# A hybrid encoder layer: TensorE of the first stage in written order, recurrence steps between thirds of projection blocks, five groups of tiles instead of six

## The chip, the core and the metric

The kernel runs on one NeuronCore of a Trainium2 chip. Its engines are TensorE (PE, with its weight loads as PEld), VectorE (DVE), ScalarE (ACT), GpSimd (POOL) and the DMA queues, of which SyncE (SP) and ScalarE issue most here. Each engine takes its instructions in order and waits at semaphores. The metric is device time in microseconds, the median of several executions. One execution was also recorded by the hardware profiler.

## What is computed

One layer of a streaming encoder, over 16 tiles of 128 frames of a new stream (tiles 0 to 15, "prompt") and one tile that holds the next 16 frames of 8 running streams (tile 16, "sample"). Cut to what matters:

```python
h = rmsnorm(x, norm_mix_pre)
P = h @ w_in                              # q, k, v, z (512 each), b, a (4 each), B, C, H (512 each)
qkv = silu(causal_dwconv(P[qkv], 4 taps)) # per channel along the frames
q, k = l2norm(q) / sqrt(128), l2norm(k)   # 4 heads of 128
# gated delta rule in chunks, S is a 128x128 state per head:
A  = strict_lower((k * beta) @ k.T * decay)
u, w = solve(I + A, [v * beta, k * beta * exp(g)])
v_new = u - w @ S
o  = (q * exp(g)) @ S + (q @ k.T * decay) @ v_new
S  = S * exp(g_last) + k_tail.T @ v_new   # the next chunk needs it
o  = rmsnorm_head(o) * silu(z)
y  = B * causal_dwconv(C * H, 3 taps)
x  = x + rmsnorm(concat(o, y) @ w_o)
x  = x + rmsnorm(SwiGLU(rmsnorm(x)))      # feed-forward, d_ff 2816
```

The chunks of the prompt are a sequence: each needs the state that the one before it leaves.

## The kernel before, in words

The work has stages: the first (projection by `w_in`, convolutions, delta rule, short convolution), the output projection by `w_o` (`o_tile`, matmuls at L818), the gate and up projections (L1034) and the down projection (L1192). Only the first and the loads of `o_tile` are touched.

**Groups and blocks.** The first stage runs over six groups of tiles, `[[0,1,16],[2,3,4],[5,6,7],[8,9,10],[11,12],[13,14,15]]`. Within a group the columns of all its tiles lie side by side (384, or 256), and the projection is 28 blocks of 128 output channels: 4 of k, 4 of v, 4 of q, 4 of z, and four times C, H, B. To keep float32 accuracy, operands are split into a high and a low part, and each block is 8 x 3 = 24 matmuls (`project`, `mm3`, L141). The weights of a block, split, are 1 MB; they are made from raw weights in the first use and kept in HBM (`weights`, L330 to L351), with three buffers on the chip.

**What follows a block.** For k, v and q (`conv_qkv`, L384 to L409): evacuate the bank (L376, in the first group L378, times the norm), copy the 3 columns of history (L393, L395), scale (L403, L405), three taps on DVE (L372), SiLU (L407), then one transposition per tile on TensorE (L428, L446, L457), and for k and q sums of squares (L413). For z a SiLU; for C, H, B products and two taps (`sc_stage`).

**Gates.** `gate_prep` makes decays and rates (Exp, Ln, Exp) and loads the decay matrices `dt` back from HBM (L319 to L325). They are scaled by the key norms in the v blocks (L451).

**The delta rule** of a group (`pair_stage`, `level_stage`, `chunk_stage`, `sample_stage`): key and query products per tile (L526, L527); the diagonal 32x32 blocks of A go to HBM (L535) and come back with one block per partition (L539); DVE inverts all of them in 31 steps of two operations (L546, L548); the result goes to HBM and back (L549, L551, L563, L569) and is joined to 128x128 inverses by small products (L575, L585, L586, L596, L601). Then, tile after tile, the recurrence: five products per tile (L641, L648, L655, L662, L667), the state update (L658), and the output's norm and transposition (`out_stage`, L624). The sample tile has products with the states of the 8 streams (L694, L696, L710).

**Order.** The program is written stage after stage, but the tile framework reorders: it lists the instructions of each engine by readiness in a timeline that it computes itself, with the written order as priority. The order on each engine is then fixed. So products of the levels and of the recurrence stand on TensorE among later projection blocks, and the last tile's recurrence of each group (`held`) is also written after the next group's inputs. Data of two groups are kept at a time (`gp`, `dp`; `dt` has 2 x 3 buffers).

**The next stage** loads `w_o` into buffers (`wor`, L794, then cast, L797, L798) that lie where the first stage's last buffers lay.

Of the kernel before, what the change touches and what calls it, by code (L numbers as in the profile page):

```python
# [9 lines left out]
F32 = mybir.dt.float32  # L10
# [7 lines left out]
P = 128  # L18
D = 1024
KD = D // P  # L20
H = 4
# [9 lines left out]
GROUPS = [[0, 1, 16], [2, 3, 4], [5, 6, 7], [8, 9, 10], [11, 12], [13, 14, 15]]  # L31
MAXT = max(len(g) for g in GROUPS)
W1 = MAXT * P
WF = W1 + NS * 3
# [3 lines left out]
NR, NKV = 3, 2  # L38
XKB = 4
NWB = 12  # L40
# [32 lines left out]
def kernel(  # L73
# [34 lines left out]
    mixd = [dram.tile([P, KD, P], F32, name=f"mixd{t}") for t in range(NT)]  # L108
# [37 lines left out]
    with ExitStack() as ph:  # L146
# [15 lines left out]
        S = gp.tile([P, H, P], F32, tag="S", name="S_init", bufs=2)  # L162
        V.memset(S, 0.0)
        junkq = gp.tile([P, P], BF16, name="junkq")
        junko = gp.tile([P, P], BF16, name="junko")

# [3 lines left out]
        dp = inner.enter_context(tc.tile_pool(name="dp", bufs=1))  # L170
        hp = inner.enter_context(tc.tile_pool(name="hp", bufs=KD + 3))
        wp = inner.enter_context(tc.tile_pool(name="wp", bufs=2))
        cp = inner.enter_context(tc.tile_pool(name="cp", bufs=2))

        def spread(r, n):
            c = n * P
            rg = cp.tile([P, W1], F32, tag="xk", name="rg", bufs=XKB)
# [8 lines left out]
        def x_prep(tiles):  # L186
            n = len(tiles)
            c = n * P
            ss = small.tile([P, MAXT], F32, tag="xss", name="xss")
            s2 = small.tile([P, MAXT], F32, tag="xs2", name="xs2")  # L190
            for i, t in enumerate(tiles):
                for q in range(2):
                    xt = cp.tile([P, D // 2], F32, tag="x", name="xt")
                    with tc.issue_after(wloads[-20 + 2 * i + q].ins):
                        nc.sync.dma_start(out=xt, in_=x[t, :, q * 512:(q + 1) * 512])
                    if q:
                        V.scalar_tensor_tensor(xt, xt, 1.0, xt, op0=ALU.mult, op1=ALU.mult, accum_out=s2[:, i:i + 1])
                    else:
                        A.activation(xt, xt, AF.Square, accum_out=ss[:, i:i + 1])
            V.tensor_add(ss[:, :n], ss[:, :n], s2[:, :n])  # L200
            r = rstd(small, ss[:, :n], n, 1.0 / D, EPS, "x")
            rb = spread(r, n)
            hi, lo = [], []
            for k in range(KD):
                xk = cp.tile([P, W1], F32, tag="xk", name="xk", bufs=XKB)
                with tc.issue_after(wloads[-11 + k].ins):
                    nc.sync.dma_start(out=xk[:, :c], in_=xT[k, :, tiles[0] * P:tiles[0] * P + c])
# [1144 lines left out]
```

## Time and profile before

| | us |
|---|---|
| median of 3 runs (2606.47 to 2608.23) | 2608.04 |
| span of the profiled execution | 2604.1 |
| start of groups 2 to 6 (their first projection matmul) | 171.3, 362.7, 518.6, 677.6, 801.2 |
| last projection matmul of the first stage | 955.9 |
| first matmul of the output projection | 969.8 |
| first matmul of the feed-forward | 1192.8 |

The span is from the first to the last instruction of the profiled execution; the runs were timed from outside. How to read the profile's lines: a group of instructions is given as line, engine, operation, `out<-in` by the program's names and shapes, then the count, busy time in microseconds and mean nanoseconds of one, and last the idle time of the engine just before them with what ended it. SPq and ACTq are instructions that issue DMAs. A row of a window gives the stretch, its length, and for each engine its busy time and number of instructions, then the granted clock of TensorE (1.00 is full speed), the DMA share and GB/s. Waits are put down to the semaphore that came last.

### The profile page before, as it was taken

The numbers are of one execution on the slowest core, as the hardware profiler recorded it, in microseconds if no ns is written. First come the engines' busy times: TensorE is split into PE (matmuls) and PEld (weight loads), VectorE is DVE, ScalarE is ACT, GpSimd is POOL, SyncE is SP. The second block draws the span as 40 slices with busy tenths as digits, with TensorE's granted clock in tenths as the row PEclk, the third lists the DMA queues.
The fourth block names the chain that finished last, engine by engine and source line by source line (L and its number), as shares of the span: only waits on it lengthen the run. The fifth ranks groups of instructions, "written<-read, shape, count | busy, mean of one in ns | idle before, by whom it ended". The sixth has DMA issues, their size and how long they took to land.

```text
span 2604.1 us, 41820 instructions
## 1 busy us (share of the span) xinstructions
PE 2507.8 (96%) x15061; PEld 2337.2 (90%) x15061; DVE 1741.0 (67%) x3502; ACT 1060.3 (41%) x2570; POOL 632.7 (24%) x580
## 2 busy tenths in 40 slices
PE   8989999999999999999999999999999999999998
PEld 7978899999888988788999999999999988787786
DVE  6876666666586655777888864544655554677588
ACT  6546145162656423444434442222433335333343
POOL 3221101010120101214556610000000035455563
PEclk9999999999999989999999999999999999999999
DMA  7966575847666564678877788877988853333465
GB/s 243 308 246 224 200 280 211 271 162 261 200 225 227 192 218 145 219 235 288 301 251 265 264 273 270 273 247 240 301 270 295 271 180 103 119 121 122 129 216 185
DMA packets 320815, 589.41 MB, mean 226 GB/s; under 512 B 55532, under 2 KB 204720, under 8 KB 301792
## 3 DMA queue, kind: packets, MB, share of 16 engines
q1 hardware_dynamic: 182512, 509.28, 57.8%
q10 hardware_dynamic: 138096, 77.46, 9.9%
q8 instruction: 119, 1.95, 0.3%
q14 instruction: 88, 0.72, 0.1%
HBM read 424.60 MB, written 162.05 MB: 225 GB/s over the span
## 4 chain that ended last, share of the span: by engine, by line
PE 67%; DVE 12%; DMA 10%; ACT 5%; issue 3%; POOL 2%; ACTq 1%; SPq 0%; DVEq 0%; POOLq 0%
PE fbank L1034 30%; PE dbank L141 15%; PE fbank L1192 11%; PE tbank L818 2%; PE dbank L818 2%; DMA xt<-in_x 1%; DMA xk<-in_xT 1%; DVE acc L372 1%; POOL dw L891 1%; ACT L407 1%; DVE Ts L548 1%; DVE pr L546 1%; DMA hTd<-ht 1%; DMA partd<-pt 1%; DMA out_y<-xr 1%
## 5 line engine op out<-in xcount | busy, mean ns | idle before, releaser
L1034 PE MATMUL fbank<-xh,fw 128*128 128x384 f32 (+1 forms) x3696 | 902.1, 327 | 9.2 <-ACT m L1068 5.1
L141 PE MATMUL dbank<-hi,w 128*128 128x384 f32 (+1 forms) x2688 | 689.3, 335 | 15.1 <-ACT w L344 6.2
L1034 PEld LDWEIGHTS fbank<-xh,fw 128*128 128x128 f32 x3696 | 653.7, 189 | 11.3 <-ACT m L1068 5.9
L1034 PE MATMUL fbank<-xl,fw 128*128 128x384 f32 (+1 forms) x1848 | 603.7, 327 | 0.0
L141 PEld LDWEIGHTS dbank<-hi,w 128*128 128x128 f32 x2688 | 482.1, 192 | 22.9 <-ACT w L344 6.6
L1192 PE MATMUL fbank<-dw,as 128*128 128x512 f32 x1980 | 460.7, 394 | 7.7 <-ACT dw L889 2.5
L1192 PEld LDWEIGHTS fbank<-dw,as 128*128 128x128 f32 x1980 | 371.6, 188 | 96.5 <-DVE as L1176 3.7
L141 PE MATMUL dbank<-lo,w 128*128 128x384 f32 (+1 forms) x1344 | 446.7, 332 | 0.1
L1034 PEld LDWEIGHTS fbank<-xl,fw 128*128 128x128 f32 x1848 | 348.7, 189 | 0.0
L141 PEld LDWEIGHTS dbank<-lo,w 128*128 128x128 f32 x1344 | 257.1, 191 | 3.3 <-issue 1.2
L1176 POOL TENSOR_TENSOR as<-ar,as 128x256 fp32r<-128x256 f32 (+1 forms) x207 | 186.7, 912 | 281.9 <-ACT as L1173 281.1
L1151 DVE TENSOR_TENSOR acc<-acc,fbank 128x512 f32<-128x512 f32 x248 | 166.3, 682 | 93.6 <-PE fbank L1192 77.9
L891 POOL TENSOR_TENSOR dw<-dr,dw 128x512 fp32r<-128x512 f32 x52 | 77.0, 1493 | 483.7 <-ACT dw L889 483.5
L1173 ACT CAST as<-ar 128x256 fp32r<-128x256 f32 (+1 forms) x288 | 118.1, 427 | 186.2 <-PE fbank L1192 133.8
L1009 ACT CAST fw<-rg 128x512 fp32r<-128x512 f32 x124 | 77.4, 624 | 190.5 <-PE fbank L1034 156.5
L372 DVE SCALAR_TENSOR_TENSOR acc<-R,cw,acc 128x384 f32<-128x384 f32 (+2 forms) x216 | 132.4, 617 | 11.4 <-ACT acc L403 7.7
L346 POOL TENSOR_TENSOR w<-wr,w 128x512 fp32r<-128x512 f32 x49 | 71.7, 1464 | 240.1 <-ACT w L344 189.8
L1081 DVE TENSOR_TENSOR c<-u,fbank 128x384 f32<-128x384 f32 (+1 forms) x66 | 34.9, 528 | 102.1 <-PE fbank L1034 102.1
L1077 DVE TENSOR_TENSOR m<-m,m 128x384 f32<-128x384 f32 (+1 forms) x44 | 23.1, 526 | 98.2 <-ACT m L1070 98.1
L344 ACT CAST w<-wr 128x512 fp32r<-128x512 f32 x98 | 56.5, 615 | 69.9 <-PE dbank L141 27.1
L546 DVE TENSOR_TENSOR pr<-As,Ts 48x31 f32<-48x31 f32 (+25 forms) x186 | 66.3, 356 | 26.4 <-DMA As<-sa 22.1
L1079 ACT ACTIVATE m<-fbank 128x384 f32<-128x384 f32 (+1 forms) x66 | 31.3, 474 | 121.4 <-PE fbank L1034 114.5
(360 smaller groups left out, 3697.2 us busy)
## 6 DMA issues: line engine op xcount, KB each, us to landing
w<-wsplit SPq DMA_DIRECT2D x119, 1024.0 KB, 5.7
fw<-fsplit SPq DMA_DIRECT2D x188, 512.0 KB, 4.6
fsplit<-fw SPq DMA_DIRECT2D x94, 512.0 KB, 4.9
partd<-pt ACTq DMA_DIRECT2D x88, 384.0 KB, 5.9
rg<-in_w_gu SPq DMA_DIRECT2D x62, 512.0 KB, 3.9
wsplit<-w SPq DMA_DIRECT2D x28, 1024.0 KB, 5.5
wr<-in_w_in SPq DMA_DIRECT2D x98, 256.0 KB, 3.4
ar<-partd SPq DMA_DIRECT2D x48, 384.0 KB, 3.5
```

The source lines that it names most:

```text
L141: T.matmul(ps, l, r, start=(i == 0), stop=(i == n - 1))
L346: e.tensor_tensor(out=wl[:, c], in0=wr, in1=wh[:, c].bitcast(F32), op=ALU.subtract)
L372: V.scalar_tensor_tensor(acc, raw(d), w[:, d:d + 1], acc, op0=ALU.mult, op1=ALU.add)
L546: V.tensor_mul(p3, As[:m, j, j + 1:32].unsqueeze(2).broadcast_to([m, a, b]), Ts[:m, j, 0:b].unsqueeze(1).broadcast_to([m, a, b]))
L818: T.matmul(pss[n], m_[:, j, :], w_[k][:, n * 512:(n + 1) * 512], start=(k == 0 and ci == 0), stop=(k == KD - 1 and ci == 2))
L891: e.tensor_tensor(out=w[:, 1], in0=v, in1=w[:, 0].bitcast(F32), op=ALU.subtract)
L1009: A.copy(w[:, 0], v)
L1034: T.matmul(ps, w_[:, c], b_[k][:, :hw], start=(first and k == 0 and ci == 0), stop=(k == KH - 1 and ci == 2), skip_group_check=not first)
L1151: V.tensor_add(dst, dst, ps)
L1173: ins = A.copy(a[:, 0, :n], v)
L1176: e.tensor_tensor(out=a[:, 1, :n], in0=v, in1=a[:, 0, :n].bitcast(F32), op=ALU.subtract)
L1192: T.matmul(ps, a[:, x_, q * P:(q + 1) * P], w[:, y_], start=(start and q == 0 and ci == 0), stop=(q == c - 1 and ci == 2), skip_group_chec ...
```

## The change

1. There are five groups, `[[0,1,16],[2,3,4,5],[6,7,8,9],[10,11,12,13],[14,15]]`. Three have four tiles, so that their matmuls have 512 columns; the last has two.
2. For the whole first stage TensorE's instructions keep the order in which they are written (`tc.manual_schedule` for PE alone). The other engines and queues are ordered by the framework as before.
3. The order of blocks in a group is k, q, one C-H-B, z, v, three C-H-B (`SEQ`). Each block is cut into thirds of 9, 9 and 6 matmuls, 84 thirds a group. `plan` writes each step of gates, pairs, solve, levels, recurrence and next inputs at a numbered third; what is numbered beyond 83 runs in the next group.
4. The transpositions of a block are written after the next block's matmuls (`laters`).
5. Products of the levels and the copies and trips around them are made for all tiles of a group at once. The decay is now one masked addition per tile and an exponential per head (with the row term as bias). The copies of history moved to POOL. Two operations of the normalization of the first group merged (`rb2`).
6. Buffers hold one group at a time (`kt`, `vt`, `kT`, `qT`, `U`, `AU`, `dt`); of the next group's normalized inputs two of eight have buffers before the group ends (`NHX`).
7. The mixed outputs are stored in two arrays, `mixo` per tile and `mixs` per group and channel block, and loaded by `o_tile` with two DMAs.

The core of the diff, new code:

```python
GROUPS = [[0, 1, 16], [2, 3, 4, 5], [6, 7, 8, 9], [10, 11, 12, 13], [14, 15]]
BLOCKS = [(kind, h) for kind in "kvqz" for h in range(H)] + [(kind, b) for b in range(4) for kind in "CHB"]
SEQ = [*range(0, 4), *range(8, 12), 16, 17, 18, *range(12, 16), *range(4, 8), *range(19, 28)]
...
def plan(g, nx, events):
    ...
    if gi:
        at(2, gate_products, g)
    at(5, gate_rates, g)
    at(11, gate_sums, g)
    at(14, gate_decay, g)
    at(16, key_norms, g)
    for i in range(n):
        at(17 + i, decay_exp, g, i)
        at(17 + i, decay_scale, g, i)
        at(21 + i, pair_keys, g, i)
        at(30 + 2 * i, pair_queries, g, i)
    at(21 + n, solve_load, g)
    for b in range(4):
        at(30 + 3 * b, solve, g, range(8 * b, min(31, 8 * b + 8)))
    at(40, solve_store, g)
    at(46, level_a, g)
    at(49, level_b, g)
    at(52, level_c, g)
    at(55, level_d, g)
    hop = 2 if n == MAXT else 3
    for i in range(npr):
        t = 60 + 3 * hop * i
        thread((t, t + hop, t + 2 * hop, t + 4 * hop), chunk(g, i))
    if npr < n:
        at(58, sample_start, g, npr)
        for h in range(H):
            t = 59 + 6 * h
            thread((t, t + 3, t + 5, t + 7, t + 9), sample_head(g, npr, h))
    ...
    if nx is not None:
        for i in range(len(tiles)):
            at(36 + 4 * i, x_rows, tiles, i, nx)
        at(54, x_spread, tiles, nx)
        for k in range(NHX):
            at(62 + 6 * k, x_norm, tiles, k, nx)
            at(63 + 6 * k, x_split, tiles, k, nx)
...
region.enter_context(tc.manual_schedule(engines={mybir.EngineType.PE}))
...
for gi, tiles in enumerate(GROUPS):
    ...
    for slot, j in enumerate(SEQ):
        jj, *w = pending.pop(0)
        early = gi == 0 and slot < 2
        ps = firsts[slot] if early else psd.tile([P, 512], F32, tag="d", name="dbank")
        for s, ks in enumerate((range(0, 3), range(3, 6), range(6, 8))):
            if not early:
                matmuls(ps, w, hi, lo, c, ks)
            if s == 2:
                later = finish_block(j, ps, g)
                fetch()
                if gi == 0 and slot == 0:
                    gate_products(g)
            for f in events.pop(3 * slot + s, ()):
                f()
        while laters:
            laters.pop()()
        if later:
            laters.append(later)
    if nx is not None:
        next_rows(gi + 1, nx)
        hi, lo, rb = nx["hi"], nx["lo"], None
    events = {t - 3 * len(SEQ): f for t, f in events.items()}
```

```python
def solve_store(g):
    n, m, As, Ts = g["n"], g["n"] * 16, g["As"], g["Ts"]
    nc.sync.dma_start(out=g["sT"][:n].rearrange("t h b j i -> (t h b) j i"), in_=Ts[:m])
    V.tensor_copy(As[:m].rearrange("p j i -> p i j"), Ts[:m])
    nc.sync.dma_start(out=g["sU"][:n].rearrange("t h b j i -> (t h b) j i"), in_=As[:m])
    utd = wk.tile([P, NS * (P + LS)], F32, tag="As", name="utd")
    ...
    for d, s in ((ud, "sU"), (td, "sT")):
        nc.sync.dma_start(out=d[:, :n].rearrange("p t h c -> p (t h) c"),
                          in_=g[s][:n].rearrange("t h b j i -> (b j) (t h) i"))

def level_a(g):
    n, npr, ud, td = g["n"], g["npr"], g["ud"], g["td"]
    for b in range(4):
        r = slice(32 * b, 32 * b + 32)
        A.copy(U[r, :n, :, r], ud[r, :n])
    ps = bank()
    for i in range(npr):
        for h in range(H):
            q = (4 * i + h) * 32
            for b in (0, 64):
                r1, r2 = slice(b, b + 32), slice(b + 32, b + 64)
                T.matmul(ps[r2, q:q + 32], AU[r1, i, h, r2], td[r1, i, h, :], start=True, stop=True)
    ...

def decay_exp(g, i):
    dt = g["dt"][i]
    for h in range(H):
        A.activation(dt[:, h, :], dt[:, h, :], AF.Exp, bias=g["nG"][:, 4 * i + h:4 * i + h + 1])

def chunk(g, i):                       # a generator: each yield ends a step of the plan
    ...                                # products with S: r, o; kl
    yield
    ...                                # U r, copied to yt
    yield
    ...                                # new state, o += QK yt, norm of o
    yield
    out_turn(g, i, o)                  # transposition, product with SiLU(z), store to mixo
    yield
```

More of the change, by code (lines that the diff above doesn't have):

```diff
@@ new lines, with fetch, matmuls @@
+        order = [(j, gi) for gi in range(len(GROUPS)) for j in SEQ]
+        pending = []
+        def fetch():
+            if order:
+                j, gi = order.pop(0)
+                pending.append((j, *weights(j, gi)))
+        def matmuls(ps, w, hi, lo, c, ks):
+            wh, wl = w
+            for k in ks:
+                for l, r in ((wh, hi), (wh, lo), (wl, hi)):
+                    T.matmul(ps[:, :c], l[:, k, :], r[k][:, :c], start=(k == 0 and r is hi and l is wh), stop=(k == KD - 1 and l is wl))
```

900 lines of the change are left out of this document (460 added, 440 removed).

## The prediction

> **What bounds the kernel now.** I read the page first, then the windows, cut where the first projection matmul of each group of tiles starts, then the timeline of TensorE and of the DMA issues around the small triangular solve.
>
> ```profile
> PE 2507.8 (96%) x15061; PEld 2337.2 (90%) x15061; DVE 1741.0 (67%) x3502; ACT 1060.3 (41%) x2570; POOL 632.7 (24%) x580
> ```
>
> ```profile
> 0.00:171.30 171.30, 148.57 (x824) 140.57 (x825) 137.78 (x349) 89.72 (x210) 54.24 (x46) 0.95 0.84 289
> 171.30:362.70 191.40, 180.42 (x1231) 167.31 (x1230) 128.18 (x325) 83.79 (x229) 21.82 (x24) 0.97 0.63 221
> 362.70:518.60 155.90, 154.19 (x1161) 149.41 (x1160) 96.08 (x272) 68.08 (x199) 10.69 (x12) 0.99 0.70 238
> 518.60:677.60 159.00, 155.92 (x1108) 149.91 (x1107) 101.69 (x278) 69.26 (x197) 11.71 (x12) 0.98 0.64 215
> 677.60:801.20 123.60, 114.71 (x964) 109.86 (x964) 96.61 (x272) 70.11 (x185) 26.60 (x22) 0.97 0.62 212
> 801.20:955.90 154.70, 148.59 (x1075) 142.43 (x1076) 89.56 (x252) 68.44 (x189) 7.47 (x9) 1.00 0.62 207
> 955.90:1192.80 236.90, 224.79 (x1173) 188.73 (x1173) 155.10 (x307) 93.59 (x233) 36.86 (x47) 0.96 0.61 198
> ```
>
> Columns: the stretch, its length, busy time of PE, PEld, DVE, ACT, POOL, granted clock, DMA share, GB/s. TensorE is the bound. The first stage takes 955.9 us, the output projection 236.9 more, up to the feed-forward's first matmul at 1192.8. The change can only move that 1192.8. Busy matmuls have modelled ends, so for the work I use the spacing in stretches that hold one kind only:
>
> ```profile
> 461.07:502.43 41.36, 41.36 (x241) 41.36 (x240) 30.32 (x87) 2.66 (x8) 0.00 (x0) 1.00 0.86 277
> 789.41:800.95 11.54, 11.54 (x95) 11.54 (x96) 9.35 (x27) 3.65 (x7) 1.29 (x1) 1.00 0.66 238
> 2305.03:2387.81 82.78, 82.78 (x365) 68.32 (x364) 59.60 (x90) 28.84 (x71) 44.74 (x50) 1.00 0.37 115
> ```
>
> They hold matmuls of 384, 256 and 512 columns: about 0.173, 0.122 and 0.227 us each. A block of 24 takes 4.15 us with three tiles, 2.92 with two and, from the last row (another stage's matmuls), 5.45 with four. One recurrence product is eight instructions:
>
> ```profile
> 293.90 1.06 PE L667 MATMUL obank<-yt,dt 128*128 128x128 f32 x8
> 294.79 1.06 PE L526 MATMUL gbank<-kT 128*128 128x128 f32 x8
> ```
>
> The next eight start 0.89 us later. Thus a group of three prompt tiles needs 28 x 4.15 = 116 us of projection and, for gates, transpositions (0.11 each), pairs, levels and recurrence, about 32: 148. The third and fourth stretches took 156 and 159. The waste is 5 to 7% there and more around the first group and the two-tile group. What keeps it low is that a solve and its recurrence may run late, under the next group's projections.
>
> **The change, part by part.** *Fewer, wider matmuls.* Before: 3360 x 0.173 + 672 x 0.122 = 663 us. After: 672 x 0.173 + 2016 x 0.227 + 672 x 0.122 = 656. It saves 7 us on the path.
>
> *Work off the path.* One solve fewer takes (67.8 + 66.3)/6 = 22 us from DVE (rows below), the edge copies move to POOL, and stores to HBM become fewer and larger. DVE is 67% busy and a matmul does not wait for these: I cost them at nothing. The POOL copies are not in the trace at this size; they can run before or behind the evacuation, so between 0 and, were they on each of 60 conv chains at a tenth of a microsecond, 6 us; I take 0.
>
> *The written order.* This is the part that counts. Within a group TensorE must now do, in this order: the k and q blocks, the key products (thirds 21 to 24), the rest of the projections, and at third 46 the first level, which needs the solve. Nothing behind it may pass, so a late solve stops the engine. I split a group into three legs.
>
> *Leg 2, from the last key product to the first level*, is a chain of a store, a load, 62 dependent DVE operations, two stores and two loads. The trace has it whole:
>
> ```profile
> 106.58 1.01 ACTq L535 DMA_DIRECT2D sa<-AU  x2
> ...
> 178.46 0.44 PE L575 MATMUL gbank<-utd,AU 32*32 32x32 f32 x16
> ...
> 749.71 0.39 ACTq L535 DMA_DIRECT2D sa<-AU  x1
> ...
> 812.60 0.44 PE L575 MATMUL gbank<-utd,AU 32*32 32x32 f32 x16
> ...
> 892.95 1.76 ACTq L535 DMA_DIRECT2D sa<-AU  x4
> ...
> 930.08 0.32 SPq L549 DMA_DIRECT2D sT<-Ts  x1
> ...
> 940.56 0.44 PE L575 MATMUL gbank<-utd,AU 32*32 32x32 f32 x16
> ```
>
> From the last tile's stores (its first issue, with two tiles its last) it takes 72 us in the first group, 63 with two tiles and 47.6 with the three of the last group. The solve's arithmetic is only this:
>
> ```profile
> L372 DVE SCALAR_TENSOR_TENSOR acc<-R,cw,acc 128x384 f32<-128x384 f32 (+2 forms) x216 | 132.4, 617 | 11.4 <-ACT acc L403 7.7
> L548 DVE TENSOR_TENSOR Ts<-Ts,pr 48x31 f32<-48x31 f32 (+25 forms) x186 | 67.8, 365 | 4.1
> L546 DVE TENSOR_TENSOR pr<-As,Ts 48x31 f32<-48x31 f32 (+25 forms) x186 | 66.3, 356 | 26.4 <-DMA As<-sa 22.1
> ```
>
> 31 x (0.365 + 0.356) = 22 us per group, however many tiles. The rest is DMA trips and other work of DVE between. In the new order the solve lies under the z blocks, where DVE has little else, so I take a little over the shortest row, 49 us with four and with two tiles, and 58 for the first group, whose weights are still split on DVE. Lower bound: the arithmetic and two trips like the last one in the rows (930.08, the solve's end, to 940.56), 43. Upper: the rows, with four tiles' larger trips 53: so 43 to 53, 43 to 63, 43 to 72. What TensorE has to do meanwhile (thirds 24, 23 and 22 to 46): four tiles, 22 x 5.45/3 = 40 plus 4 for query products and transpositions, 44; first group, 23 x 4.15/3 + 3 = 35; two tiles, 24 x 2.92/3 + 2 = 25. So it waits about 5, 23 and 24 us.
>
> *Leg 1, up to the last key product.* TensorE's work with four tiles is 8.4 blocks x 5.45 = 46, gate products 16 x 0.227 = 4, transpositions 3, key products 4 x 0.89 = 4: 57. Beside it stands ScalarE:
>
> ```profile
> L413 ACT ACTIVATE junkq<-tbank 128x128 bf16<-128x128 f32 x136 | 37.5, 276 | 13.4 <-PE tbank L457 6.5 <-DVE rg L178 1.5 <-DVE sqe L615 1.0
> L407 ACT ACT_TABLE_LOAD x27 | 34.6, 1283 | 0.8 <-DVE hist L395 0.3
> L403 ACT ACTIVATE acc<-dbank,cw 128x384 f32<-128x384 f32 x48 | 28.2, 587 | 0.1
> L413 ACT ACTIVATION_READ_ACCUMULATOR junkq<-tbank 128x1 f32 x136 | 27.1, 199 | 0.0
> L376 ACT COPY R<-dbank 128x384 f32<-128x384 f32 x48 | 22.7, 473 | 6.1 <-PE dbank L141 5.9
> L451 ACT ACTIVATE dt<-dt,c 128x128 f32<-128x128 f32 x68 | 20.9, 389 | 1.5 <-DVE c L437 1.5
> ```
>
> Per k or q block with four tiles: copy, scaling and SiLU, each about 0.6 (0.47 to 0.59 at 384 columns), four sums of squares of up to 0.475, for k one more copy: 3.2 to 4.4 us; eight blocks, 30. The decay is now 16 exponentials and 16 scalings of 0.3 to 0.39: 11. Some ten table loads (Exp, Ln and SiLU alternate) at 1.28: 13. Together 54 to 60 against 57. I take 59. The Trainium skill, "ScalarE: Activation LUTs", Terms, gives about 2.7 us for a table load; by that the leg would be some 14 us longer in each of five groups. The row says 1.28 and decides. With two tiles TensorE needs 28; ScalarE has 8 x 2 for the blocks, 5 for decays, 13 for tables, 5 for raw weights, 3 for others: 42. First group: the first two blocks wait for the loads as before, and DVE needs, per block, two evacuations (about 0.7 together), three taps of 0.62 to 0.73, a weight split (0.7 to 0.96) and edge copies: 4.4 to 4.6 for each 4.15 us block. Nine blocks and the start give 76.
>
> *Leg 3, from the first level to the group's end.* Four tiles: 12.25 x 5.45 = 67, levels 7, recurrence 4 x 5 x 0.89 = 18, the rest 4, and 4 for hops and the change of group, where six of eight normalized inputs wait for buffers of the block before: 100. First group, with the sample tile's 23 of products: 93. Two tiles: 12.25 x 2.92 = 36, levels 4, recurrence 9, rest 2, hops 3: 54.
>
> *The sum.* First group 76 + 58 + 93 = 227, three groups of 59 + 49 + 100 = 208 make 624, last 42 + 49 + 54 = 145: 996 against 955.9. But before, levels and recurrence of its last tiles ran after 955.9, about 20 us of products under the output projection's start:
>
> ```profile
> 956.93 0.92 SPq L794 DMA_DIRECT2D wor<-in_w_o  x2
> ...
> 969.85 0.77 PE L818 MATMUL dbank<-woh,mh 128*128 128x512 f32 x1
> ```
>
> Its weights can load only when the stage's buffers are free, and 14 us pass to its first matmul. After the change nothing is left to fill them, though DVE, then free, shortens them to about 10. The matmuls (17 tiles x 48 x 0.227 = 185) and transpositions (14) make 199; with 10 idle, 5 at a slow clock and 9 of later waits, as now, 223 instead of 236.9. So 996 + 223 = 1219 against 1192.8: **26 us longer**. The profiled span goes from 2604.1 to 2630; the median of 2608.04 lies 3.9 above the span, so 2634.
>
> **The rivals.** *B, the solve fits (faster).* If DVE serves the solve nearly without a break and the trips are at their short end, leg 2 falls to TensorE's own 44, 35 and 25, and no wait is left at the level: 3 x 5 + 23 + 24 = 62 us less, 2572. It speaks for it that 22 us of arithmetic and two trips of some 10 us fit 44; against it, none of the three rows is under 47 us, and two tiles have 25. It decides on the sign when the five waits together are under 36 us.
>
> *C, the transposition a block later comes too soon.* Now a block's transpositions may come late. After the change they stand one block behind, 5.9 us with four tiles; copy, scaling, three taps and SiLU take at least 0.6 + 0.7 + 2.3 + 0.6 = 4.2 (taps at 0.77, an estimate from 0.617). One other DVE and ScalarE operation in between is allowed, a table load with it is not. At 1.3 us more in 12 blocks of three groups it costs 45: 2679.
>
> *D, the clock.*
>
> ```profile
> PE tbank L141 <- DMA utd<-sT: 9.6, 1, 9.6
> ```
>
> ```profile
> 165.00:175.00 10.00, 4.03 (x13) 3.30 (x14) 5.04 (x10) 3.91 (x11) 2.35 (x4) 0.50 0.89 294
> ```
>
> The one long wait of now, 9.6 us on the solve's result, lies in a stretch with the clock at 0.50, and work after it ran at half speed for some 4 us. If each of five waits at the level does that, 2 to 3 us are lost each: 12 in all, 2646. The Trainium skill, "TensorE: Matmul & The Clock Gate", Part 1, says that an idle window of about 3.4 us throttles and about 3.4 us of activity releases; by it five waits lose five times 1.7, some 8 us.
>
> *E, the order is not what limits.* If the waits of before stay as they are, only 7 us of matmuls and a little at the start of the next stage change: 2597.
>
> **How the numbers follow.** Chances: the forecast 0.46, B 0.24, C 0.15, D 0.08, E 0.07. The forecast's own range, from the bounds of leg 2 (three times -5 to +4, -15 to +14, -6 to +14) with some of the errors cancelling, is 2610 to 2673. The range 2570 to 2680 takes in most of B and half of C. A measurement of this kernel tells 0.2%, 5 us, from no change. Faster by more: B and most of E, 0.30. Within: the rest of E and the forecast's low edge, 0.05. Slower: 0.65.
>
> **What would show it.** The 512-column projection matmuls should start 0.227 us apart. TensorE's largest waits should be at the first level (level_a), released by the load of the solved blocks, some 5 us with four tiles and over 15 in the first and last groups; if they are under 7 on average, B is right. Waits of the transpositions for SiLU of over 1 us in most k, v and q blocks would be C. The last projection should end near 996 and the feed-forward start near 1219. The prediction is wrong in its main step if the store-to-level chain takes under 42 us.

## The result, and the profile after

The changed kernel takes 2726.25 us (median of 4 runs, 2721.49 to 2729.33) against 2607.26 of the kernel before (4 runs, 2603.69 to 2608.23): ratio 1.0466, 95% interval 1.0447 to 1.0484. It is slower by 119 us; forecast were 26, and the range ended at 2680. The profiled execution's span is 2726.4 us, with a mean granted clock of 0.961 (0.984 before).

The page's first part, of the kernel after: busy time, share of the span, instructions.

```profile
PE 2509.9 (92%) x14366; PEld 2254.1 (83%) x14366; DVE 1672.9 (61%) x2986; ACT 1047.8 (38%) x2464; POOL 657.1 (24%) x724
```

TensorE is as long busy as before (2507.8) and the span is 122 us longer, so most of the loss is waiting. (The run no_order below shows that some of the busy time is loss too.) The prediction cut a group into three legs: to the last key product, to the first level, to the group's end. The windows of the kernel after, cut there (columns as before: stretch, length, PE, PEld, DVE, ACT, POOL, clock, DMA share, GB/s): leg 1 of the first group; the three legs of the third group; the three of the last.

```profile
7.60:88.30 80.70, 61.32 (x293) 54.65 (x294) 47.28 (x111) 52.91 (x136) 23.97 (x31) 0.83 0.56 198
...
479.80:560.20 80.40, 64.71 (x292) 49.66 (x291) 35.49 (x66) 55.88 (x148) 8.28 (x19) 0.89 0.46 157
560.20:613.00 52.80, 44.28 (x213) 36.86 (x213) 29.16 (x80) 8.81 (x24) 0.37 (x2) 0.95 0.66 205
613.00:711.40 98.40, 98.39 (x740) 84.09 (x741) 47.44 (x89) 25.10 (x60) 10.39 (x22) 0.97 0.45 153
...
943.00:999.30 56.30, 38.40 (x243) 34.65 (x243) 28.74 (x63) 38.51 (x103) 11.95 (x21) 0.79 0.43 145
999.30:1046.00 46.70, 25.73 (x215) 25.19 (x214) 30.33 (x78) 8.44 (x25) 4.61 (x7) 0.84 0.52 167
1046.00:1102.60 56.60, 53.32 (x518) 51.82 (x518) 33.07 (x61) 20.80 (x56) 13.27 (x21) 0.95 0.37 127
```

Beside the forecast, in us (the other groups of four tiles are within 3 of the third; the first group's leg 1 includes the 7.6 of the start):

| leg | forecast first / four tiles / last | measured |
|---|---|---|
| 1 | 76 / 59 / 42 | 88.3 / 83.1, 80.4, 80.8 / 56.3 |
| 2 | 58 / 49 / 49 | 59.5 / 52.8, 52.8, 52.7 / 46.7 |
| 3 | 93 / 100 / 54 | 98.0 / 98.1, 98.4, 98.1 / 56.6 |
| output projection | 223 | 214.7 |

Leg 1 is 94 us over its forecast, leg 2 is 10 and leg 3 is 2, and the output projection 8 under: together the 98 us by which the feed-forward starts late (1317.3 for 1219).

TensorE's waits in the kernel after (what waits, for whom: us in total, times, longest):

```profile
PE gbank L574 <- DMA utd<-sT: 68.0, 5, 23.9
PE tbank L325 <- ACT qT L318: 32.8, 7, 7.9
PE dbank L281 <- ACT hi L206: 31.4, 7, 7.2
PE tbank L325 <- ACT kT L318: 15.2, 11, 3.0
...
PE dbank L951 <- ACT mh L945: 9.8, 1, 9.8
```

The first row is the level (L574) waiting for the solved blocks: the 62 us of the forecast. `hi` (L206) is the next group's normalized input: 28 of the 31.4 us are the four changes of group, for which the sum had at most 4 each. `qT` and `kT` are SiLUs that a transposition (L325) waits for; the sum had nothing for them. The last row is the output projection's start, 9.8 for a forecast 10.

**The change of group.** SyncE's DMA issues at the end of the second group, in the kernel after (start, time over which they issue, line, what, count):

```profile
479.95 0.32 SPq L251 DMA_DIRECT2D w<-wsplit  x1
480.32 10.94 SPq L236 DMA_DIRECT2D xk<-in_xT  x6
```

The group's last matmuls run up to 479.8. The weight load needs the buffer that they free; the six input loads are written behind that load, so they issue after it, and the first is there at 486.5. TensorE waits 6.8 us, then for one split after another, and at half speed, as the granted clock of the stretch (0.50) shows:

```profile
485.40:495.40 10.00, 6.65 (x13) 3.93 (x13) 7.21 (x11) 3.99 (x6) 0.00 (x0) 0.50 0.45 153
```

The first block of the group takes 21.4 us (row below), of which matmuls at 0.227 us would fill 5.45 and gate products 3.6.

**The q blocks.** ScalarE's windows inside the third group's leg 1, kernel after (stretch, length, ACT busy, clock, DMA share, GB/s):

```profile
479.80:501.20 21.40, 7.06 (x17) 0.76 0.53 178
...
535.00:552.00 17.00, 16.88 (x50) 0.80 0.47 169
```

It is idle for two thirds of the first block and has no gap in the 17 us in which the second q block's SiLU is late. Its timeline there:

```profile
534.28 0.59 ACT L289 COPY R<-dbank 128x512 f32<-128x512 f32 x1 [2.13 <-POOL rt L506]
...
537.03 1.28 ACT L495 ACTIVATE dt<-dt,nG 128x128 f32<-128x128 f32 x4
...
544.09 1.28 ACT L318 ACT_TABLE_LOAD   x1
545.38 0.63 ACT L318 ACTIVATE qT<-acc 128x512 f32<-128x512 f32 x1
```

The second q block's SiLU (545.38) stands behind the decays, exponentials and scalings, from 537.03 on and two table loads; TensorE's transposition waits 6.0 us for it. VectorE in the same stretch:

```profile
536.15 1.35 DVE L490 TENSOR_TENSOR dt<-dt,cst 128x512 f32<-128x512 f32 x2 [4.09 <-DMA dt<-grow]
537.42 0.75 DVE L285 SCALAR_TENSOR_TENSOR acc<-R,cw,acc 128x512 f32<-128x512 f32 x1
...
541.12 0.69 DVE L490 TENSOR_TENSOR dt<-dt,cst 128x512 f32<-128x512 f32 x1 [1.67 <-DMA dt<-grow]
```

Mask additions that wait for the decay rows stand in front of the taps (L285) that the SiLU needs. So four causes could share leg 1: late loads, a chain of queues, ScalarE's load, or the written order as such. The experiments take them apart.

### The profile page after: what moved, and what is told of

The parts are those of the page before. It is cut to its first block, busy times and chain, and to the rows that moved or that the text cites. A ratio compares the mean times of both kernels' runs of the same rounds, so it can differ in the third digit from the quotient of the medians.

```text
span 2726.4 us, 39699 instructions
## 1 busy us (share of the span) xinstructions
PE 2509.9 (92%) x14366; PEld 2254.1 (83%) x14366; DVE 1672.9 (61%) x2986; ACT 1047.8 (38%) x2464; POOL 657.1 (24%) x724
## 4 chain that ended last, share of the span: by engine, by line
PE 72%; DVE 9%; DMA 8%; ACT 6%; issue 3%; POOL 1%; SPq 0%; ACTq 0%; DVEq 0%; POOLq 0%
PE fbank L1167 31%; PE dbank L281 16%; PE fbank L1325 12%; PE tbank L951 3%; PE dbank L951 3%; DMA xk<-in_xT 2%; DMA xt<-in_x 1%; DVE Ts L549 1%; DVE pr L547 1%; DMA sU<-As 1%; DMA utd<-sT 1%; ACT L318 1%; ACT dt L495 1%; ACT junkq L330 1%; PE tbank L325 1%
## 5 line engine op out<-in xcount | busy, mean ns | idle before, releaser
L281 PE MATMUL dbank<-hi,w 128*128 128x512 f32 (+2 forms) x2240 | 686.6, 379 | 40.8 <-ACT hi L206 31.4
L281 PEld LDWEIGHTS dbank<-hi,w 128*128 128x128 f32 x2240 | 427.4, 198 | 98.9 <-ACT hi L206 34.8
L281 PE MATMUL dbank<-lo,w 128*128 128x512 f32 (+2 forms) x1120 | 417.0, 372 | 4.6 <-DVE lo L207 4.6
L281 PEld LDWEIGHTS dbank<-lo,w 128*128 128x128 f32 x1120 | 222.2, 198 | 38.0 <-DVE lo L207 13.9
L285 DVE SCALAR_TENSOR_TENSOR acc<-R,cw,acc 128x512 f32<-128x512 f32 (+2 forms) x180 | 131.2, 730 | 97.0 <-ACT acc L314 91.4
L261 POOL TENSOR_TENSOR w<-wr,w 128x512 fp32r<-128x512 f32 x49 | 64.8, 1322 | 117.4 <-ACT w L259 110.0
L259 ACT CAST w<-wr 128x512 fp32r<-128x512 f32 x98 | 56.3, 616 | 57.1 <-PE dbank L281 31.3
L1143 POOL TENSOR_TENSOR fw<-rg,fw 128x512 fp32r<-128x512 f32 x44 | 69.5, 1579 | 30.8 <-ACT fw L1142 30.7
```

Source lines behind the costliest of these rows:

```text
L261: e.tensor_tensor(out=wl[:, c], in0=wr, in1=wh[:, c].bitcast(F32), op=ALU.subtract)
L281: T.matmul(ps[:, :c], l[:, k, :], r[k][:, :c], start=(k == 0 and r is hi and l is wh), stop=(k == KD - 1 and l is wl))
L285: V.scalar_tensor_tensor(acc, raw(d), w[:, d:d + 1], acc, op0=ALU.mult, op1=ALU.add)
L1143: e.tensor_tensor(out=w[:, 1], in0=v, in1=w[:, 0].bitcast(F32), op=ALU.subtract)
```

## The experiments

All times are medians; ratios are against the kernel before, timed on the same chip. The changed kernel stands at 2726.25.

| run | edit to the changed kernel | us | ratio, 95% interval |
|---|---|---|---|
| no_order | written order taken away | 2578.9 | 0.9891, 0.9869 to 0.9913 |
| no_order_six | no_order, six groups | 2625.3 | 1.0079, 1.0058 to 1.0099 |
| no_order_x | no_order, input loads earlier | 2575.2 | 0.9883, 0.9865 to 0.9901 |
| no_order_all3 | no_order, three edits | 2580.5 | 0.9911, 0.9890 to 0.9933 |
| x_early | input loads earlier | 2693.8 | 1.0337, 1.0308 to 1.0365 |
| q_lag2 | q transposed two blocks behind | 2698.6 | 1.0353, 1.0328 to 1.0378 |
| levels_later | levels six thirds later | 2698.4 | 1.0355, 1.0328 to 1.0383 |
| all3 | these three | 2641.7 | 1.0136, 1.0115 to 1.0156 |
| warm | matmuls in the level waits | 2716.0 | 1.0416, 1.0395 to 1.0437 |
| decay_pool | decay scalings on GpSimd | 2720.3 | 1.0445, 1.0426 to 1.0463 |
| gates_early | decay rows earlier | 2721.8 | 1.0445, 1.0413 to 1.0478 |
| silu_first | exponentials behind the SiLU | 2727.0 | 1.0461, 1.0445 to 1.0476 |
| q_chain | gates_early, silu_first, the power later | 2718.9 | 1.0441, 1.0418 to 1.0464 |
| q_chain_pool | q_chain and decay_pool | 2702.3 | 1.0372, 1.0352 to 1.0393 |
| all4 | all3 and gates_early | 2626.2 | 1.0084, 1.0061 to 1.0106 |
| all4_silu | all4 and silu_first | 2636.5 | 1.0110, 1.0090 to 1.0130 |

### Is it the written order?

```diff
-        region.enter_context(tc.manual_schedule(engines={mybir.EngineType.PE}))
```

> The written order of TensorE is taken away: the framework orders its instructions again as it does in the kernel before; the groups of four, the new stages and everything else of the change stay. Theory A (the written order is the loss: nothing behind a late step may pass): the waits at the first level (69.8 us), on late SiLUs (45) and much of the half-speed work (15) go, and the time comes to 2600 to 2640. Theory B (the first leg's loss comes from the new stages themselves, the late input loads and ScalarE in the q blocks, whatever the order): the level waits go, but the four group changes still cost some 9 us each and the rest of ScalarE's lateness stays: 2650 to 2690. Theory C (four tiles and single buffers are what makes it slow): 2700 or more.

2578.9: theory A, 21 us under its range, and 147 us less than with the order, more than the whole loss. TensorE's waits in no_order:

```profile
PE dbank L281 <- DMA w<-wsplit: 16.3, 12, 4.1
...
PE gbank L574 <- DMA utd<-sT: 5.1, 2, 4.0
PE tbank L325 <- ACT qT L318: 5.0, 4, 2.6
```

The level waits 5.1 us instead of 68, `qT` 5.0 instead of 32.8, and no row for `hi` is left among the large ones. TensorE's same 14366 instructions are busy for 2480.2 us here, 2509.9 in the kernel after: some 30 of the 152 us between the two spans are instructions that last longer. The lower clock in the kernel after (0.961 for 0.989) fits that; no run separates it. How it gets there is in the counts of projection matmuls (L281) between the starts of successive first levels. The windows of that line in no_order, and the first two of the same kind in the kernel after:

```profile
0.00:192.40 192.40, 145.26 (x716) 132.24 (x716) 0.96 0.78 268
192.40:401.00 208.60, 155.45 (x635) 117.10 (x634) 0.99 0.59 198
401.00:571.60 170.60, 126.53 (x505) 94.58 (x505) 0.97 0.53 182
571.60:760.80 189.20, 152.00 (x627) 114.92 (x626) 1.00 0.55 185
760.80:946.20 185.40, 136.95 (x880) 120.09 (x879) 1.00 0.54 182
```

```profile
0.00:147.70 147.70, 81.89 (x378) 74.19 (x378) 0.84 0.65 223
147.70:381.70 234.00, 154.73 (x672) 124.20 (x672) 0.94 0.58 192
```

At 24 to a block, the first level of the first group comes after 29.8 blocks in no_order and after 15.75 in the written order. Summed up, the later ones come after 56.3, 77.3, 103.5 and 140 blocks, against 43.75, 71.75, 99.75 and 127.75: 4 to 14 blocks later, different in each group. The written order's place is the same in every group and early.

### What are the five groups worth?

```diff
-GROUPS = [[0, 1, 16], [2, 3, 4, 5], [6, 7, 8, 9], [10, 11, 12, 13], [14, 15]]
-MAXT = max(len(g) for g in GROUPS)
+GROUPS = [[0, 1, 16], [2, 3, 4], [5, 6, 7], [8, 9, 10], [11, 12], [13, 14, 15]]
+MAXT = 4
```

> Without the written order and with the six groups of the kernel before (0 1 16, 2-4, 5-7, 8-10, 11-12, 13-15), in buffers still sized for four tiles; the new stages, stores and planned places stay. Theory 1 (the 26 us under before come from five groups: 7 us of wider matmuls and one solve, one group change and one first leg less): about 2600 to 2610, that is before's time. Theory 2 (they come from the other parts: edge copies on GpSimd, fewer stores, the new order of blocks): within 8 us of 2579.

2625.3, outside both theories: five groups are worth 46 us, not 26, and with six groups the other new parts, their plan and buffers made for five, cost about 20. TensorE's largest wait in no_order_six is for weights:

```profile
PE dbank L281 <- DMA w<-wsplit: 32.4, 17, 4.4
```

against 16.3 in no_order. That is about 16 of the 46; the rest was not told apart.

### The three places in the written order

x_early:

```diff
-            with tc.issue_after(wloads[-1].ins):
+            with tc.issue_after(wloads[-4].ins):
                 nc.sync.dma_start(out=xk[:, :c], in_=xT[k, ...])
```

> The loads of the next group's inputs that were queued on SyncE behind the newest weight load now follow a weight load three blocks older; nothing else changes. Theory (the group change is late because these six loads stand behind a weight load that itself waits for the group's last block): the first block of each later group, now 21.4 us instead of the 5.45 of its matmuls plus 3.6 of gate products, falls to 11 to 14, so 7 to 10 us go in each of four group changes: 2726 - 28 to 40 = 2686 to 2698. Rival 1 (the splits are late anyway, because their buffers come free only in the group's last block, or because VectorE and ScalarE are behind): the wait for hi and lo stays and under 8 us go, 2718 or more. Rival 2 (the time gained is waited out again at the first level, because the solve's chain is not on TensorE's clock): the same, under 8 us, with level waits grown by 7 each.

2693.8, 32.5 less: the theory. The first block of the third group in x_early (all engines' columns):

```profile
471.90:482.10 10.20, 9.84 (x46) 6.46 (x45) 7.61 (x15) 4.32 (x13) 1.38 (x3) 1.00 0.68 238
```

The same 46 matmuls take 10.2 us instead of 21.4, at a clock of 1.00 instead of 0.76, and the level wait did not grow (67.7).

q_lag2:

```diff
-                while laters:
-                    laters.pop()()
+                due = 3 * len(SEQ) * gi + 3 * slot
+                while laters and laters[0][0] <= due:
+                    laters.pop(0)[1]()
                 if later:
-                    laters.append(later)
+                    laters.append((due + (6 if BLOCKS[j][0] == "q" else 3), later))
```

> The transpositions of the four q blocks are written two blocks behind instead of one; those of k and v stay. Theory (TensorE waits for the SiLU of a q block that ScalarE, full of decay exponentials and table loads, delivers late): the waits of the transposition bank on qT, 34.0 us in all, go: 2726 - 25 to 34 = 2692 to 2701. Rival (they were beside the path: the solve's chain starts after the decays and key products, and those wait for ScalarE too, so that the first level is waited for by as much more): the wait of the level on the solved blocks grows from 69.8 to over 90 and the time stays within 8 us of 2726.

2698.6, 27.7 less: the theory. Its waits on `qT` and at the level:

```profile
PE gbank L574 <- DMA utd<-sT: 72.7, 5, 23.3
...
PE tbank L325 <- ACT qT L318: 3.8, 2, 2.1
```

29 us of waits on `qT` went and the level took 5 back.

levels_later:

```diff
+            off = 6 if gi else 0
-            at(46, level_a, g)           # and level_b, level_c, level_d
+            at(46 + off, level_a, g)
...
-                t = 60 + 3 * hop * i
+                t = 60 + off + 3 * hop * i
```

> In all groups but the first, the four levels and the recurrence are written six thirds (two blocks) later. Theory (each level wait is TensorE arriving too early, by 9 us in groups of four tiles and 19 in the last): six thirds are 10.9 us with four tiles and 5.8 with two, so the waits go in three groups (27 us) and fall by 6 in the last; with half of the slow-clock work behind them some 4 more: 2726 - 32 to 38 = 2688 to 2694. Rival (the products moved into the next group stand where that group's gates, waits for inputs and k blocks are, and lengthen it, or the tail of the last group is exposed): gain under 15, 2711 or more, with no level wait left but longer group starts.

2698.4, 27.8 less: the theory's side, 4 us over its range. The level waits fall to 39.0 (3 times), and a new one of 13.6, out_turn waiting for VectorE's `o`, appears.

all3 has the three edits together.

> The three edits together in the written order: input loads three weight loads earlier, q transpositions two blocks behind, levels and recurrence six thirds later in all groups but the first. Theory (the written order loses at three separate places, each of which the others do not cover): the gains found one by one, 32.5, 27.7 and 27.8 us, add up: 2726 - 88 = 2638, still slower than 2605, since k transpositions (15), the first level of the first and last group (24 and 13) and the half clock stay. Rival (they hide each other: an earlier leg meets the next wait): the level waits come back in the groups of four tiles, and the time is 2655 to 2680.

2641.7: 84.6 less, against 88.0 for the three added up. The three losses are separate and add. What is left, in all3:

```profile
PE gbank L574 <- DMA utd<-sT: 38.1, 2, 23.3
PE tbank L325 <- ACT vraw L318: 17.7, 5, 8.0
PE obank L640 <- DVE o L635: 14.6, 6, 6.0
```

The first and the last group's level, and v transpositions and normalized outputs that now come due too early: each edit moves a place, and other places then wait.

no_order_x and no_order_all3 put the edits under the framework's order.

> Without the written order, and with the six input loads three weight loads earlier. Theory 1 (the framework's order hides the group change already: there is no wait for hi left in that run): within 6 us of 2579. Theory 2 (the loads still stand in front of weights there: 16 us of waits for the split weights at the group starts): up to 15 us less, 2564. Theory 3 (earlier loads take the buffers and the queue away from the last blocks' weights): 2585 or more.

> Without the written order, with all three edits (input loads earlier, q transpositions two blocks behind, levels and recurrence planned six thirds later). Theory 1 (the framework's order already puts later work in front of what is late, so the edits, worth 85 us in the written order, are worth nothing here): within 8 us of 2577. Theory 2 (planned places still set the framework's priorities and take away some of the 68 us of waits that are left in its first stage): 2555 to 2570.

2575.2 and 2580.5 against 2578.9: nothing, theory 1 in both. What costs 85 us in a written order costs nothing where later work may pass.

### The clock behind the waits

In front of the levels, with the results thrown away:

```diff
+            hi, c = g["hi"], n * P
+            for m in range({3: 130, 4: 34, 2: 140}[n]):
+                T.matmul(ps[:, :c], hi[m % KD][:, 0:P], hi[(m + 1) % KD][:, :c], start=True, stop=True)
```

> The changed kernel as it is, with matmuls written in front of each first level whose results are thrown away, to fill most of the wait there: 130 of 384 columns (22.5 us) in the first group, 34 of 512 (7.7 us) in the others of four tiles, 140 of 256 (17 us) in the last; they read the normalized inputs, which are there. Theory (the rival on the clock: a wait leaves TensorE at half speed for some us behind it; from the spacing of instructions in the changed kernel 2.4, 1.1, 1.5, 1.5 and 2.1 us are lost behind the five levels, 8.6 in all): 2726 - 6 to 10 = 2716 to 2720. Rival (the half speed behind these waits costs nothing, since what follows waits for ScalarE and VectorE anyway): within 4 us of 2726. If the matmuls overrun the wait or slow the solve down: above 2726.

2716.0, 10 less, with an interval of some 6 us to either side (five runs, 2709.2 to 2727.2): the theory. In its profiled execution leg 3 took 96.8, 96.6, 96.6, 95.7 and 56.1 us in the five groups, 7.4 less in all than in the kernel after. That execution's total, 2727.2, does not show the gain: what stands behind the first stage, which the edit leaves alone, took 7 us longer in it. Windows of the kernel after around the third group's level show what went:

```profile
604.50:608.00 3.50, 0.00 (x0) 0.00 (x0) 0.00 (x0) 0.00 (x0) 0.00 (x0) 1.00 0.89 330
608.30:618.20 9.90, 5.19 (x72) 4.48 (x73) 0.70 (x2) 5.90 (x11) 0.52 (x1) 0.50 0.40 57
618.60:625.00 6.40, 6.40 (x152) 5.15 (x152) 3.08 (x6) 1.93 (x4) 0.30 (x2) 1.00 0.70 248
```

TensorE is idle from 604.5 to 613.0; the clock halves 3.5 to 4 us into that and is whole again only 5 us after work restarts.

### What makes the q block's SiLU late?

Five runs go to this. decay_pool takes work off ScalarE:

```diff
-            for h in range(H):
-                A.mul(dt[:, h, :], dt[:, h, :], g["c2"][:, 4 * i + h:4 * i + h + 1])
+            G.tensor_tensor(out=dt, in0=dt, in1=bc(g["c2"][:, 4 * i:4 * i + 4]), op=ALU.mult)
```

> The changed kernel in its written order, with the scaling of the decays (16 instructions of 0.39 us on ScalarE per group of four tiles) as one GpSimd instruction for each tile (such a one, kl, took 1.12 us). Theory (in the q blocks ScalarE has no slack: 16.88 us busy of 17.0 in the stretch in which TensorE waits for qT, so each us taken off it there comes off the wait): of the 6.2 us per group most that stand ahead of the late SiLU go, 4 to 6 in the four groups of four or three tiles, 2 in the last, and the level does not wait longer: 2726 - 16 to 25 = 2701 to 2710. Rival (the late SiLU waits for VectorE's taps or for table loads, or the scaling on GpSimd comes later than on ScalarE and delays the solve): within 8 us of 2726, with longer waits at the first level.

gates_early lands the rows earlier:

```diff
-            at(11, gate_sums, g)
-            at(14, gate_decay, g)
+            at(8, gate_sums, g)
+            at(11, gate_decay, g)
```

> The changed kernel in its written order, with the sums of the gates three thirds earlier (8 for 11) and the decay rows' trip through HBM too (11 for 14). Theory (what makes a q block's SiLU late is a line of in-order queues behind that trip: VectorE's mask additions wait for the decay rows, landed 536.2 to 541.1 in the third group, and stand in front of the q block's taps, and ScalarE's decays stand in front of its SiLU; 5.4 us earlier rows let both go before the taps come): the waits on qT, 33 us, fall to 15 or less, the level waits stay: 2726 - 15 to 28 = 2698 to 2711. Rival (ScalarE's work in these blocks, decays, sums of squares, copies and five or six table loads, is too much wherever the rows land, or the earlier gates cost waits of their own): within 8 us of 2726.

2720.3 and 2721.8, 6.0 and 4.4 less: in both the rival's size. In gates_early the third group's rows were there 7 us sooner after the group's start, and ScalarE's timeline reads:

```profile
525.55 1.28 ACT L495 ACTIVATE dt<-dt,nG 128x128 f32<-128x128 f32 x4
526.86 1.28 ACT L318 ACT_TABLE_LOAD   x1
528.15 0.63 ACT L318 ACTIVATE qT<-acc 128x512 f32<-128x512 f32 x1
```

The exponentials just came sooner too, and stand again in front of the SiLU. So silu_first turns that order round:

```diff
-            A.activation(dst[:, :pc], acc[:, :pc], AF.Silu)
+            now["silu"] = A.activation(dst[:, :pc], acc[:, :pc], AF.Silu)
...
-            for h in range(H):
-                A.activation(dt[:, h, :], ..., AF.Exp, ...)
+            with tc.issue_after(now["silu"].ins):
+                for h in range(H):
+                    A.activation(dt[:, h, :], ..., AF.Exp, ...)
```

> The changed kernel in its written order, with each tile's four decay exponentials put, on ScalarE, behind the newest SiLU written by then. Theory (the late SiLU is a matter of ScalarE's order: the exponentials of all tiles, about 5 us with two table loads around them, are ready earlier and stand in front of the SiLU of the second q block): the waits on qT, 33 us, fall to 15 or less, since the exponentials then share the next block's slack, and with fewer changes of table: 2726 - 13 to 28 = 2698 to 2713; as the decays come later, the level waits may grow by up to 3 each. Rival (ScalarE is full in these blocks whatever its order): the wait moves to the third q block, within 8 us of 2726.

2727.0: nothing, the rival. In the third group the wait of 6.0 became one of 3.8 at the same block (its taps still wait for the rows) and one of 2.0 at the last q block, behind the decays. q_chain was to cut all three queues: gates_early, silu_first, and GpSimd's power (L506), ahead of the edge copy that the evacuation waits for, written at third 24 instead of 16. q_chain_pool takes the scalings off ScalarE as well.

> The changed kernel in its written order with three edits together: decay rows three thirds earlier, the exponentials behind the newest SiLU, and GpSimd's power for the values' norms at third 24 instead of 16. Theory (three in-order queues one behind the other, so that cutting one leaves the next): the waits on qT fall from 33 to 12 or less and those on kT from 15 to 10: 2726 - 18 to 28 = 2698 to 2708. Rival (ScalarE has more work in the q blocks than the blocks last, so the order only moves the wait to the third q block): qT waits over 20 us, the time within 10 us of 2726.

> The same with the decay scalings on GpSimd (one instruction of about 1.1 us per tile for four of 0.39 on ScalarE). Theory of the chain: hardly better than q_chain, by up to 5 us. Rival (ScalarE's load): q_chain gains little, this one 15 to 25 more, since 5 us less load per group of four tiles meet a wait of some 6: about 2700.

2718.9 and 2702.3: 7.4 and 24 less, the rival on load in both. Waits on `qT` in decay_pool, gates_early, silu_first, q_chain and q_chain_pool:

```profile
PE tbank L325 <- ACT qT L318: 26.8, 8, 7.8
```

```profile
PE tbank L325 <- ACT qT L318: 28.9, 7, 6.2
```

```profile
PE tbank L325 <- ACT qT L318: 29.8, 13, 4.7
```

```profile
PE tbank L325 <- ACT qT L318: 32.7, 11, 5.5
```

```profile
PE tbank L325 <- ACT qT L318: 19.6, 8, 5.4
```

The three edits of order only move the wait between q blocks (11 waits for 7, none over 5.5); load alone is hidden by the order (26.8). Only both together bring it down, so ScalarE's load is part of the cause. That ScalarE has more to do in the q blocks than the blocks last is not shown, and q_chain is no clean test of order. Its third group has, on GpSimd, on ScalarE, and in ScalarE's window over the q blocks (stretch, length, ACT busy, clock, DMA share, GB/s):

```profile
525.02 3.33 POOL L514 TENSOR_TENSOR rt<-ssk,half 128x16 f32<-128x16 f32 x1 [3.62 <-DVE ssk L506]
```

```profile
527.94 0.63 ACT L318 ACTIVATE qT<-acc 128x512 f32<-128x512 f32 x1 [4.27 <-DVE acc L285]
```

```profile
515.00:553.00 38.00, 29.59 (x90) 0.96 0.46 165
```

Only TensorE is in written order: the power, written 8 thirds later, starts 52.5 us after the group's first matmul, where it started 51.1 after it, and still ends right before an edge copy (528.30). VectorE's taps still stand among mask additions that wait for the decay rows (the last at 526.48), and ScalarE waits 4.3 us for them; in all it is idle for 8.4 of these 38 us. How much of the late SiLU is load and how much the queues stays open.

### Further along

all4 is all3 with gates_early; all4_silu adds silu_first.

> The three edits of before together (2641.65 in their run), and the sums of the gates and the decay rows three thirds earlier too. Theory (with q transposed two blocks behind, the rows' trip no longer holds TensorE in the q blocks, but the solve starts after it, and that still shows at the first level and in the 10 us of waits on kT): 5 to 15 us less, 2627 to 2637. Rival (nothing is left on the path from the rows on): within 5 us of 2642.

> The four edits together (2626.22 in their run) and the exponentials behind the newest SiLU. Theory (with q transposed two blocks behind nothing on TensorE waits for that SiLU; only fewer table loads are left to gain, and later decays to lose): within 6 us of 2626. Rival (the exponentials' place still matters for k or for the start of the solve): 8 us or more away, either way.

all4: 2626.2, 15.4 under all3: the theory, at the end of its range. all4_silu: 2636.5, the rival: with later exponentials a new row appears, the key products waiting for a bank that VectorE frees once the decay is there:

```profile
PE gbank L517 <- DVE AU L518: 13.4, 4, 7.7
```

So the best written order found here is still 0.8% slower than before, and the best kernel is the change without it: no_order at 0.989 and no_order_x at 0.988, not told apart.

## Why the prediction was wrong

**Direction: right, and the mechanism at the level.** Nothing may pass a late step, and so the new order loses. But it loses at more places than the sum had, and the range ended 46 us short.

**Leg 2: right.** The wait at the level was forecast as 3 x 5 + 23 + 24 = 62 us and is 68.0; in the groups of four it is near 9 each instead of 5, in the last 19 instead of 24. Rival B (the solve fits) is out.

**Leg 3 and the output projection: right in size**, within 2 us in sum and 8; in leg 3 partly by luck, since its forecast held 4 us per group for the change of group, which in the trace falls into the next group's leg 1. "14 us shorten to about 10" came out at 9.8. A block of 24 matmuls of 512 columns lasts 5.4 us where nothing disturbs it, as forecast.

**Leg 1: the step that failed**, 94 us too short, in two terms of the sum. The first, booked in leg 3, is "4 for hops and the change of group, where six of eight normalized inputs wait for buffers". The buffers were seen; that the six loads are queued behind a weight load which itself waits for the group's last block was not. SyncE's queue at this place stood nowhere in the sum. It cost 32.5 us by x_early.

The second is ScalarE "54 to 60 against 57. I take 59". The load was right: it was busy 55.88 us in that leg. But the leg took 80.4, since the larger of two totals is a lower bound only. ScalarE did 7 us in the first 21 and then 16.88 in 17, and TensorE, in order, could not lend it time from one to the other. By q_lag2 this cost 27.7 us. The two make 60 of the 94; of the other 34, 15 stand as waits on `kT`, and the rest was not taken apart.

Here the Trainium skill, "ScalarE: Activation LUTs", Terms, with 2.7 us for a table load, would have made the leg 73 and so come nearer. It would have done so for the wrong reason: in the gates_early rows above, the exponentials end at 526.83 and the SiLU starts at 528.15, so the switch takes 1.3 us, as the row of before said.

**Rivals were priced as alternatives and were parts of a sum.** C (transpositions come too soon) was given 45 us; `qT` and `kT` wait 32.8 + 15.2 = 48. That the two numbers agree is luck, for its place was other than said: not 1.3 us in most blocks, but 5 to 8 in each group's q blocks, mostly in one wait, and 2 to 5 for k. D (the clock) was given 12; warm gives 7 to 10 for the waits at the level, and the half speed behind the other waits (0.50 at the change of group, row above) was in no rival. Forecast 2634, C's 45, D's 12 and the 32 of the group change make 2723, against 2726. D's sentence on the Trainium skill's rule ("TensorE: Matmul & The Clock Gate", Part 1) came to 8 us; the trace at the third group's level, 3.5 to 4 us until the clock halves and 5 until it is whole, is a little above that page's 3.4 and 3.4.

**E (the order doesn't limit)** describes no_order: 2597 forecast, 2578.9 measured. The matmuls' 7 us were taken as the five groups' whole worth; by no_order_six the five groups are worth 46.

**"I take 0" for the copies on GpSimd** was not quite right either: in the third group ScalarE's evacuation of a q block waited 2.1 us for GpSimd (timeline above), which the profile puts down to the power that runs ahead of the copy; the copies themselves took 0.2 us each. It lies inside the q chain, and alone it was not measured.

## What to carry to other kernels

When an engine is put in written order, every place where an input can be late is a term of its own, and here the three that were moved added up: go along the order step by step with each producer's queue, instead of comparing engines' totals over a leg. Follow a moved DMA to the instruction that it is queued behind, and ask what that one waits for. Where a scheduler can choose the order, count how many blocks late it puts the late steps: here it was 4 to 14 blocks later than the plan written by hand, and different for each group. And look in the trace whether an edit moved what it was written to move: GpSimd's power stayed where it was.

## What the runs showed of the hardware

A power on GpSimd is dear: on 128x16 elements (L506) it took 3.38 us in the third group (GpSimd's spans are rough), three times a multiplication of 128x512 (L647) with 32 times the elements. POOL's timeline of the kernel after:

```profile
530.86 3.38 POOL L506 TENSOR_TENSOR rt<-ssk,half 128x16 f32<-128x16 f32 x1 [2.15 <-DVE ssk L505]
534.19 0.18 POOL L304 COPY R<-hist 128x3 f32<-128x3 f32 x1
534.34 1.04 POOL L647 TENSOR_TENSOR kl<-kt,tl 128x512 f32<-128x512 f32 x1
```

The 0.18 us copy between them starts only when the power ends, and so does a block's evacuation on ScalarE, at 534.28 after a wait of 2.1 us.
